# Holding splits and weight work behind evictions, and moving sums and a norm, in a hybrid GLA, mLSTM and ConvFFN layer

## The chip, the cores and the metric

One core of a Trainium2 chip runs the whole layer. The metric is device microseconds of one execution, the median of several runs. Beside the runs there is one profiled execution with a trace of every engine: TensorE (PE, with its weight loads PEld), VectorE (DVE), ScalarE (ACT), GpSimd (POOL) and SyncE (SP), whose queue issues most DMAs.

## The reference

One decoder layer over 1024 tokens and 16 prepended learned tokens, 1024 channels, in float32:

```python
def mixer_block(h, w_in, b_in, ...):
    proj = h @ w_in + b_in
    (g_q, g_k, g_v, g_r, g_lr, m_q, m_k, m_v, m_o, m_i, m_f, gate_a, gate_b) = split(proj)
    o_gla = head_rms(gla_chunked(g_q, g_k, g_v, log_a), gla_norm) * silu(g_r)        # 4 heads
    o_ml = head_rms(mlstm_chunked(mq, mk, m_v, m_i, log_sigmoid(m_f)), ml_norm) * sigmoid(m_o)  # 4 heads
    y = sigmoid(gate_a) * (o_gla @ w_branch_gla) + sigmoid(gate_b) * (o_ml @ w_branch_ml)
    return y @ w_out

def conv_ffn(h, w_up, conv_w, conv_b, w_down):
    gate, up = split(causal_dwconv(h @ w_up, conv_w, conv_b))
    return (silu(gate) * up) @ w_down

h = h + mixer_block(rms_norm(h, norm_mix), ...)
h = h + conv_ffn(rms_norm(h, norm_ffn), ...)
return rms_norm(h, norm_final)[:, N_META:, :]
```

## The kernel before

**Precision and products.** Every float32 operand of a matmul is held as two parts: H, a rounded copy made by ScalarE (`activation(h, raw, AF.Copy)`), and L, the remainder made by VectorE (`tensor_tensor(l, raw, h, subtract)`). This pair of instructions is called a split here. A product takes three matmuls, H·H, H·L and L·H. The gate, up and down stages also save one product in eight with a scheme of sums of blocks: seven products of half size stand for eight, and their operands are sums and differences of blocks of tokens and of weights.

**Stages in order.** (1) Norm and transposes of x. (2) Eight heads s = 0..7 (four GLA, four mLSTM); a head's projections are interleaved on PE with the chunk steps of the head before, its products with v are evicted by VectorE at L205, its output rows go through `post(s, ...)`. (3) The gate stage, 14 weight pairs q = 0..13, two token halves p = 0, 1 each. (4) The merge, with the branch weights (bg, bm). (5) The output projection (po). (6) The up stage, 22 weight pairs. (7) The down stage, two rounds r of two phases. (8) The final norm, per round, and the stores of the output.

**What sets an order.** The program is written as Python that emits instructions. Each engine runs its own list in order; a scheduler makes that list from the order in the program, from when operands are expected, and from priorities (`hp(...)`). `tc.issue_after(ins)` adds an edge: what is emitted inside it comes after `ins` in the list. A tile with a tag takes one of `bufs` places of that tag; a new tile waits until the last reader of the old one in its place is done.

**The gate stage.** `piece(...)` (L987 on) runs one half p of a pair: products V and X into two PSUM banks, evicted by ScalarE L1003 (V into g1) and VectorE L1004 (X + g1); products Y and Z; a second product into the same bank X, evicted by ScalarE L1011 (u2) and added by VectorE L1012 and L1013; then products into Y and Z again, L1018 and L1019. It is a generator: the caller puts the tail of one piece behind the first products of the next. `gate_weights(q)` (L1043 and L1060 to L1067) loads two weight tiles gw and makes sums and splits of them in four steps, called by `weights_step`. `token_blocks` loads the four token blocks TB for both halves p from DRAM (tsc); `token_splits(p)` (L1099, L1100) splits them. In before `token_splits(1)` and the first step of weights q = 1 are emitted between the pieces of q = 0, without an edge.

**The merge.** The eight tiles of o_gla are loaded and split into ogH, ogL by `load_o` (L1192, L1193). The branch weights come through the prefetcher `U`, whose `get` calls `prep` (L102 load, L106 and L107 split), whenever it is that the scheduler finds room.

**The up stage.** `combos(i)` (L1340 to L1357) makes, for the i-th quarter of tokens, combinations t12 and t34 of eight rows each and splits them into BH and BL tiles (Br for blocks, Bt for combinations). The last, i = 3, is emitted while the first pieces already run. `gate_pair(q)` (L1427 to L1439) does the convolution and the product silu(gate)·up, and stores a and its sums s to DRAM (adr).

**The down stage.** `fill(i, ...)` (L1588 transfers in one chain on SP, L1609 and L1610 splits) brings step i's weights (raw, and sums from tdn) and rows (adr) into one of several places; `down` (L1630) runs 24 or 18 matmuls on them. `middle` and `finish` add the banks into accs at L1697; `finish` also squares (L1711), takes roots (VectorE L1715 and L1716, GpSimd L1718), scales with the final norm (L1723) and stores (L1725).

**The token sums.** `token_sums(k)` (L464 to L472) makes, for k = 0..3 during heads s = 3..6, the sums of the token blocks that the gate stage needs: full rows of H + L, their differences, all on GpSimd, then eight DMAs from GpSimd's queue to tsc. It is called at the end of `post(s)`, with rows a and b in tag "r" and t in tag "of". `half_load` and `half_sums` (L485 to L493), which follow, make sums of the down weights. The root of head s, the tile rs{s}r, is a power on GpSimd (L93); ScalarE's scaling of the head's output (L568, L569) waits for it.

Of the kernel before, what the change touches and what calls it, by code (L numbers as in the profile page):

```python
# [45 lines left out]
def hybrid_kernel(ctx, tc, x, meta, norm_mix, w_in, b_in, gla_w_gate, gla_b_gate, gla_norm,  # L46
# [47 lines left out]
        return r  # L94


    behind = []

    def prep(src, shape, name):

        raw = wp.tile(shape, F32, name="wr_" + name, tag="wr", bufs=2)
        nc.sync.dma_start(raw, src)  # L102
        wH = wp.tile(shape, F32R, name="wH_" + name, tag="wH")
        wL = wp.tile(shape, F32R, name="wL_" + name, tag="wL")
        with tc.issue_after(behind[0].ins) if behind else nullcontext():
            nc.scalar.activation(wH, raw, AF.Copy)  # L106
        nc.vector.tensor_tensor(wL, raw, wH.bitcast(F32), OP.subtract)  # L107
        return wH, wL
# [236 lines left out]
    norm_x(0)  # L345
    norm_x(1)
    U.get(0, 0)
    behind.append(norm_x(2)[1])
    U.get(1, 0)
    behind.clear()  # L350
    load_x(3)
    for dst, ap in small[4:9]:
        nc.sync.dma_start(dst, ap)
# [104 lines left out]

    def token_sums(k):

        a, b = (hd.tile([P, T], F32, name=f"x{i}{k}", tag="r", bufs=2) for i in "ab")
        t = hd.tile([P, T], F32, name=f"tx{k}", tag="of", bufs=2)
        for y, i in ((a, k), (b, k + 4)):
            nc.gpsimd.tensor_tensor(y[:, :NP], xH[:, i, T0:].bitcast(F32), xL[:, i, T0:].bitcast(F32), OP.add)  # L464
        first, second = slice(0, 514), slice(512, NP)
        t1, t2 = t[:, 0:514], t[:, 520:1034]
        for dst, x, y in ((t1, a[:, second], a[:, first]), (t2, b[:, second], t1),
                          (a[:, second], b[:, second], a[:, second]), (b[:, first], b[:, first], t2)):
            nc.gpsimd.tensor_tensor(dst, x, y, OP.subtract)
        for i, src in enumerate((t1, t2, a[:, second], b[:, first])):  # L470
            for p in range(2):
                stored = nc.gpsimd.dma_start(tsc[p][i, :, k], src[:, 258 * p:258 * p + 258 - 2 * p])  # L472
        return stored
# [90 lines left out]
    def post(s, o, om, sc, ncols):  # L564

        h = s % 4
        g = "g" if s < 4 else "m"
        for c in range(NC):  # L568
            nc.scalar.activation(o(c), o(c), AF.Copy, scale=sc[:, c + 1:c + 2])  # L569
        nc.scalar.activation(om, om, AF.Copy, scale=sc[:2, 0:1])  # L570
        for _ in range(3 if s != 3 else 6):
            yield
        for j in range(2):
            of = hd.tile([P, T], F32, name=f"of{s}_{j}", tag="r", bufs=2)
            for gi in range(2):
# [12 lines left out]
        if 3 <= s < 7:  # L588
            for _ in range(4 if s == 3 else 0):
                yield  # L590
            stored = token_sums(s - 3)
            if s < 6:
                for _ in range(2):
                    yield
                with tc.issue_after(stored.ins):
                    t = half_load(wp, "gst")
                for _ in range(3):
                    yield
                half_sums(*t)

    def state(name):
# [377 lines left out]
    def product(out, a, b, n, start, stop):  # L981
        for k in range(4):
            for j, (x, y) in enumerate(((a[0], b[0]), (a[0], b[1]), (a[1], b[0]))):
                nc.tensor.matmul(out[:, :n], x[:, k, :], y[:, k, :], start=start and k == 0 and j == 0,  # L984
                                 stop=stop and k == 3 and j == 2, skip_group_check=True)

    def piece(pool, name, p, us_, u2, A, B):  # L987
# [12 lines left out]
        prod(V, "A12", "B21", True, True)  # L1000
        prod(X, "A11", "B11", True, True)
        with hp(PRI_E):
            nc.scalar.activation(g1, V[:, :n], AF.Copy)  # L1003
            nc.vector.tensor_tensor(g1, X[:, :n], g1, OP.add)  # L1004
        yield
        prod(Y, "S1", "T1", True, True)
        prod(Z, "S3", "T3", True, True)
        yield
        prod(X, "S2", "T2", False, True)
        with hp(PRI_E):  # L1010
            nc.scalar.activation(u2, X[:, :n], AF.Copy)  # L1011
            nc.vector.tensor_tensor(e2, Y[:, h2], u2[:, h2], OP.add)  # L1012
            nc.vector.tensor_tensor(e2, Z[:, h2], e2, OP.add)  # L1013
# [81 lines left out]
    def token_splits(p):  # L1095
        c = (slice(0, W0), slice(W0, 514))[p]
        for i in (0, 2, 1, 3):
            h, l = (t[:, :, c] for t in TB[i])
            nc.scalar.activation(h, l.bitcast(F32), AF.Copy)  # L1099
            nc.vector.tensor_tensor(l, l.bitcast(F32), h.bitcast(F32), OP.subtract)  # L1100
# [42 lines left out]
    for q in range(NG):  # L1143
        gu[q] = [row(f"gu0{q}", "u0", 2), row(f"gu1{q}", "o1" if q >= NK and q % 2 else "u1")]
        for p in range(2):
            g = piece(psG, f"g{q}", p, gu[q], u2, WP[q], gate_block)
            next(g)
            if p == 1:
                weights_step(q + 1)
            next(g)  # L1150
            if p == 1:
                weights_step(q + 1)
            if behind_:
                next(behind_)
            if p == 0:
                weights_step(q)
                if q:
                    gate_finish(q - 1)
                else:
                    token_splits(1)  # L1160
                weights_step(q + 1)
# [20 lines left out]
    def load_o(g, pool, tags, queue):  # L1182
# [6 lines left out]
        for k in range(NK):  # L1189
            h, l = (t[p, k // 4][:, k % 4, :NP] for p in "HL")  # L1190
            last = queue.dma_start(l.bitcast(F32), otd[g][k])
            nc.scalar.activation(h, l.bitcast(F32), AF.Copy)  # L1192
            nc.vector.tensor_tensor(l, l.bitcast(F32), h.bitcast(F32), OP.subtract)  # L1193
        return tuple([t[p, k // 4][:, k % 4, :] for k in range(NK)] for p in "HL"), last

    ubg = [u_cm(w_bg, P * j, f"bg{j}") for j in range(NK)]
    ubm = [u_cm(w_bm, P * j, f"bm{j}") for j in range(NK)]
# [25 lines left out]
        nc.gpsimd.dma_start(yg[j], gsc["a"][j])  # L1223

    merge_tile(0)
    og, loaded = load_o("g", r2, "O", nc.gpsimd)
    for j in range(NK):
        y = yg[j]
        if j < NK - 1:
# [4 lines left out]
            nc.vector.tensor_tensor(th(y), pt, th(y), OP.mult)  # L1234
        if j == 1:
            with tc.issue_after(opened.ins), tc.issue_after(loaded.ins):
                om_, loaded = load_o("m", r1b, "R", nc.gpsimd)
        for i in ((), (), (5, 6, 7), (6, 7), (6, 7), (), (), ())[j]:
            half_sums(*half_load(r2, f"Y{i}"))

# [103 lines left out]
    def combos(i):  # L1344
# [6 lines left out]
        nc.vector.tensor_tensor(t12[:, 4:8], B[:, 4:8], t12[:, 0:4], OP.subtract)  # L1351
        nc.vector.tensor_tensor(t34[:, 0:4], B[:, 4:8], B[:, 0:4], OP.subtract)
        nc.vector.tensor_tensor(t34[:, 4:8], A[:, 4:8], t12[:, 4:8], OP.subtract)
        for dst, r0, n, src in ((Br, 0, 8, A), (Br, 8, 4, B[:, 4:8]), (Bt, 0, 8, t12), (Bt, 8, 8, t34)):
            h = dst["H", p][:, r0:r0 + n, c0:c0 + w]
            nc.scalar.activation(h, src, AF.Copy)
            x = nc.vector.tensor_tensor(dst["L", p][:, r0:r0 + n, c0:c0 + w], src, h.bitcast(F32), OP.subtract)  # L1357
# [347 lines left out]
    def finish(r, j):  # L1705
# [21 lines left out]
        with hp(400 if j == 0 else 200):  # L1727
# [8 lines left out]
            if not end:  # L1736
# [37 lines left out]
            if (r, ph, m) == (1, 0, 1):  # L1774
                ring.extend(back)

    back = []
    i = FIRST
    while i < len(seq):
        r, ph, m = seq[i]  # L1780
# [53 lines left out]
```

## Time and profile before

| | us |
|---|---|
| runs | 1926.53, 1923.99, 1923.37 |
| median | 1923.99 |
| profiled execution, its own time | 1925.63 |
| its span from first to last instruction | 1923.6 |
| mean granted clock of TensorE | 0.995 |

How to read what follows. A row of the timeline is: start in us, duration in us, engine, line, operation, output<-input, partitions x elements, xcount, and in brackets how long the engine sat idle before it and who released it. A row of the waits is: who waited, for whom, us in total, times, longest. A row of windows is: start:end, length, PE's busy time with its matmuls, the granted clock of TensorE (1.00 is full), the DMA engines' share, GB/s. An engine with a q behind its name (SPq, ACTq) is issuing a DMA.

### The profile page before, as it was taken

What the parts mean: (1) busy time and instruction counts of PE and PEld (TensorE: products, weight loads), DVE (VectorE), ACT (ScalarE), POOL (GpSimd) and SP (SyncE); (2) the same over time, 40 slices, a digit from 0 to 9 for tenths busy, and PEclk for the clock granted to TensorE, in tenths of its full rate; (3) what the DMA queues carried; (4) which work ended last, traced back from release to release, by engine and by line L of the source; (5) the groups of instructions that cost most, each with busy time, mean ns of one, the idle gap of its engine ahead of it and who ended that gap; (6) DMA issues with size and microseconds to landing.
All of it is one profiled execution on the core that took longest, in us unless ns stands there. A gap on an engine that the chain in (4) does not pass through costs nothing. (4 is left out here: it accounts for less than half of the span.)

```text
span 1923.6 us, 32692 instructions
## 1 busy us (share of the span) xinstructions
PE 1867.8 (97%) x13377; PEld 1785.1 (93%) x13377; DVE 1199.3 (62%) x1775; ACT 853.9 (44%) x1369; POOL 413.5 (21%) x463
## 2 busy tenths in 40 slices
PE   8999999999999899999899999999999999999998
PEld 8989989999889899999899999999999999987776
DVE  6456556455552356565442555688888788886776
ACT  5345555545453433332331234544343443455564
POOL 3101111140553001124272610012222222200000
PEclk9999999999999999999999999999999999999999
DMA  5111021042332936666873653323433334288794
GB/s 166 34 36 58 12 69 50 20 136 91 99 100 89 212 84 165 165 167 174 286 260 112 219 177 121 123 79 108 129 119 100 106 109 127 82 305 332 265 369 161
DMA packets 221824, 270.02 MB, mean 140 GB/s; under 512 B 13742, under 2 KB 177088, under 8 KB 221675
## 3 DMA queue, kind: packets, MB, share of 16 engines
q1 hardware_dynamic: 200603, 199.93, 33.5%
q0 software_dynamic: 16928, 57.76, 9.2%
q10 hardware_dynamic: 4144, 10.26, 1.5%
q8 instruction: 105, 1.72, 0.4%
q14 instruction: 44, 0.36, 0.1%
HBM read 198.33 MB, written 69.57 MB: 139 GB/s over the span
## 5 line engine op out<-in xcount | busy, mean ns | idle before, releaser
L491 POOL TENSOR_TENSOR ts<-ts 128x256 f32<-128x256 f32 x88 | 75.6, 866 | 43.0 <-DMA ts<-in_ffn_w_down_dram 41.0
L1394 POOL TENSOR_TENSOR SB<-SA,rg 128x512 f32<-128x512 f32 x20 | 31.8, 1591 | 236.6 <-issue 123.7
L201 PE MATMUL pv<-wH_gv,xH 128*128 128x256 f32 x256 | 75.3, 294 | 0.0
L201 PE MATMUL pv<-wH_mv,xH 128*128 128x256 f32 x256 | 75.1, 293 | 0.0
L1481 PE MATMUL po<-wH_wo,yH 128*128 128x256 f32 x256 | 72.8, 284 | 0.1
L201 PE MATMUL pv<-wH_gv,xL 128*128 128x256 f32 x256 | 72.5, 283 | 0.0
L201 PE MATMUL pv<-wL_gv,xH 128*128 128x256 f32 x256 | 72.1, 282 | 0.0
L1481 PE MATMUL po<-wL_wo,yH 128*128 128x256 f32 x256 | 71.7, 281 | 0.3 <-DVE wL_wo L107 0.3
L1481 PE MATMUL po<-wH_wo,yL 128*128 128x256 f32 x256 | 72.0, 282 | 0.0
L201 PE MATMUL pv<-wL_mv,xH 128*128 128x256 f32 x256 | 72.0, 281 | 0.0
L201 PE MATMUL pv<-wH_mv,xL 128*128 128x256 f32 x256 | 71.9, 281 | 0.0
L704 POOL TENSOR_TENSOR pk<-pk,kT 128x256 f32<-128x256 f32 (+1 forms) x24 | 30.6, 1277 | 175.0 <-ACT pk L702 164.4
L1209 PE MATMUL bg<-ogH,wH_bg 128*128 128x342 f32 x192 | 61.8, 323 | 3.9 <-ACT ogH L1192 3.9
L1429 DVE SCALAR_TENSOR_TENSOR cv<-u,fc,cv 128x1024 f32<-128x1024 f32 x44 | 65.3, 1483 | 0.4
L1376 POOL TENSOR_TENSOR A<-u2raw,A 128x512 fp32r<-128x512 f32 x20 | 43.9, 2195 | 92.5 <-ACT A L1375 92.5
L1209 PE MATMUL bg<-ogL,wH_bg 128*128 128x342 f32 x192 | 61.9, 324 | 0.7 <-DVE ogL L1193 0.7
L1209 PE MATMUL bg<-ogH,wL_bg 128*128 128x342 f32 x192 | 61.8, 323 | 0.0
L1209 PE MATMUL bm<-omH,wH_bm 128*128 128x342 f32 x192 | 61.4, 320 | 0.0
L1209 PE MATMUL bm<-omH,wL_bm 128*128 128x342 f32 x192 | 61.3, 319 | 0.0
L1209 PE MATMUL bm<-omL,wH_bm 128*128 128x342 f32 x192 | 61.2, 319 | 0.0
L205 DVE TENSOR_TENSOR v<-pv,bB 128x256 f32<-128x256 f32 x64 | 26.8, 419 | 54.4 <-PE pv L201 54.3
L1718 POOL TENSOR_TENSOR fr<-fv,mhalf 128x1 f32<-128x1 f32 x8 | 6.4, 806 | 231.9 <-DVE fv L1716 231.9
(754 smaller groups left out, 7508.9 us busy)
## 6 DMA issues: line engine op xcount, KB each, us to landing
gw<-in_w_in_dram SPq DMA_DIRECT2D x26, 512.0 KB
ts<-in_ffn_w_down_dram POOLq DMA_DIRECT2D x44, 256.0 KB, 3.6
tdn<-ts POOLq DMA_DIRECT2D x44, 256.0 KB, 2.8
rg<-in_ffn_w_up_dram SPq DMA_DIRECT2D x22, 512.0 KB
ru<-in_ffn_w_up_dram SPq DMA_DIRECT2D x22, 512.0 KB
adr<-s SPq DMA_DIRECT2D x40, 256.0 KB
rd<-in_ffn_w_down_dram SPq DMA_DIRECT2D x20, 512.0 KB
do<-tdn SPq DMA_DIRECT2D x18, 512.0 KB
```

The lines of the kernel that those rows point to most:

```text
L201: nc.tensor.matmul(pt[:, :DV], a[:, k, t0:t0 + P], b[:, k % 4, :], start=(i == 0), stop=(i == 3 * NK - 1))
L205: nc.vector.tensor_tensor(vt[:n, c, :DV], pt[:n, :DV], bB[:n, :], OP.add)
L491: nc.gpsimd.tensor_tensor(t[:, o], t[:, a], t[:, b], OP.subtract)
L704: eng.tensor_tensor(e, e, k, OP.mult)
L1209: nc.tensor.matmul(pt[:, i, :n], a[:, k, :], b[k][:, t0:t0 + n], start=(k == 0 and j == 0), stop=(k == NK - 1 and j == 2))
L1376: eng.tensor_tensor(l, src, h.bitcast(F32), OP.subtract)
L1394: late.tensor_tensor(sb[:, 0:4], sa[:, 0:4], rg[:, 0:4], OP.subtract)
L1429: nc.vector.scalar_tensor_tensor(y, u[:, j:SEQ + j], fc[:, j, jj:jj + 1], y, OP.mult, OP.add)
L1481: nc.tensor.matmul(pt[:, :DV], a, b[:, k % 4, :], start=(k == 0 and i == 0), stop=(k == NK - 1 and i == len(terms) - 1))
L1718: nc.gpsimd.tensor_tensor(rs, v, mhalf, OP.pow)
```

## The change

It moves work in time; the arithmetic is the same.

- The list `behind` becomes `held`, set by `hold(...)`; `prep` puts the first half of a split after the held instruction.
- `piece` remembers its evictions in `evicted` (V: L1003, X: L1004, U: L1011, Z: L1013 by the lines of before).
- Gate stage: `token_splits(1)` is cut in two. Blocks 0 and 2 come after the evictions of V and X of the first piece, blocks 1 and 3 and the first step of weights q = 1 after U and Z; the next steps of q = 1 also after Z.
- Merge: the second use of the branch-weight prefetcher comes after the last U, the third after the last split of o_gla.
- Up stage: `combos(3)` makes six splits in place of four, in another order.
- From up to down: `fill(0)` comes after the last U.
- Token sums: two rows in tag "of" in place of two in "r" and one in "of"; eight operations of 514 columns in place of two of 1026 and four of 514; called at the start of `post(s)`. The half loads and half sums go into the loop over j.
- Final norm: roots, scaling and stores of round 0 are put off to step k = 2 of the next phase.

```diff
+    held = []
+    def hold(*ins):
+        held[:] = ins
     def prep(src, shape, name):
...
-        with tc.issue_after(behind[0].ins) if behind else nullcontext():
+        with tc.issue_after(held[0]) if held else nullcontext():
             nc.scalar.activation(wH, raw, AF.Copy)
...
     def token_sums(k):
-        a, b = (hd.tile([P, T], F32, name=f"x{i}{k}", tag="r", bufs=2) for i in "ab")
-        t = hd.tile([P, T], F32, name=f"tx{k}", tag="of", bufs=2)
-        for y, i in ((a, k), (b, k + 4)):
-            nc.gpsimd.tensor_tensor(y[:, :NP], xH[:, i, T0:].bitcast(F32), xL[:, i, T0:].bitcast(F32), OP.add)
...
+        a, b = ([t[:, :514], t[:, 520:1034]] for t in (
+            hd.tile([P, T], F32, name=f"x{i}{k}", tag="of", bufs=2) for i in "ab"))
+        def whole(dst, i, c0):
+            nc.gpsimd.tensor_tensor(dst, xH[:, i, c0:c0 + 514].bitcast(F32), xL[:, i, c0:c0 + 514].bitcast(F32), OP.add)
+        def less(dst, x, y):
             nc.gpsimd.tensor_tensor(dst, x, y, OP.subtract)
+        whole(a[1], k, second)
+        whole(a[0], k, first)
+        less(b[0], a[1], a[0])
+        whole(b[1], k + 4, second)
+        less(a[1], b[1], a[1])
+        less(b[1], b[1], b[0])
+        whole(a[0], k + 4, first)
+        less(a[0], a[0], b[1])
...
     def post(s, o, om, sc, ncols):
+        if 3 <= s < 7:
+            stored = token_sums(s - 3)
         for c in range(NC):
...
                 if gi == 0:
                     yield
+                    if 3 <= s < 6:
+                        if j == 0:
+                            with tc.issue_after(stored.ins):
+                                t = half_load(wp, "gst")
+                        else:
+                            half_sums(*t)
...
-        if 3 <= s < 7:
-            for _ in range(4 if s == 3 else 0):
-                yield
-            stored = token_sums(s - 3)
...
             if p == 0:
                 weights_step(q)
                 if q:
                     gate_finish(q - 1)
+                    weights_step(q + 1)
                 else:
-                    token_splits(1)
-                weights_step(q + 1)
+                    with tc.issue_after(evicted["V"]), tc.issue_after(evicted["X"]):
+                        token_splits(1, (0, 2))
             next(g)
+            if p == 0 and q == 0:
+                opening = dict(evicted)
+                with tc.issue_after(evicted["U"]), tc.issue_after(evicted["Z"]):
+                    token_splits(1, (1, 3))
+                    weights_step(1)
...
     merge_tile(0)
-    og, loaded = load_o("g", r2, "O", nc.gpsimd)
+    og, loaded, split = load_o("g", r2, "O", nc.gpsimd)
+    hold(evicted["U"])
+    U.get(ubg[0], 1)
+    hold(split.ins)
+    U.get(ubg[0], 2)
+    hold()
...
+        if i == 3:
+            jobs = ((Br, 0, 8, A), (Bt, 0, 4, t12[:, 0:4]), (Bt, 8, 4, t34[:, 0:4]), (Bt, 4, 4, t12[:, 4:8]),
+                    (Br, 8, 4, B[:, 4:8]), (Bt, 12, 4, t34[:, 4:8]))
...
             used[i] = ring[i](i)
-            fill(i, used[i])
+            with tc.issue_after(evicted["U"]) if i == 0 else nullcontext():
+                fill(i, used[i])
...
             if not end:
-                whole(1)
+                if r:
+                    whole(1)
+                else:
+                    later.append(whole)
                 return
...
+        if later and k == 2:
+            for whole in later:
+                for x in range(2):
+                    whole(x)
+            later.clear()
```

More of the change, by code (lines that the diff above doesn't have):

```diff
@@ L94, in rstd_of @@
         return r
-    behind = []
+    held = []
+    def hold(*ins):
+        held[:] = ins
     def prep(src, shape, name):
@@ L347, in hybrid_kernel @@
     U.get(0, 0)
-    behind.append(norm_x(2)[1])
+    hold(norm_x(2)[1].ins)
     U.get(1, 0)
-    behind.clear()
+    hold()
     load_x(3)
@@ L459, in token_sums @@
     def token_sums(k):
-        a, b = (hd.tile([P, T], F32, name=f"x{i}{k}", tag="r", bufs=2) for i in "ab")
-        t = hd.tile([P, T], F32, name=f"tx{k}", tag="of", bufs=2)
-        for y, i in ((a, k), (b, k + 4)):
-            nc.gpsimd.tensor_tensor(y[:, :NP], xH[:, i, T0:].bitcast(F32), xL[:, i, T0:].bitcast(F32), OP.add)
[L465 to L470, printed above, removed]
+        a, b = ([t[:, :514], t[:, 520:1034]] for t in (
[3 more added lines that the diff above has]
+        def less(dst, x, y):
+            nc.gpsimd.tensor_tensor(dst, x, y, OP.subtract)
+        first, second = T0, T0 + 512
+        whole(a[1], k, second)
[6 more added lines that the diff above has]
+        less(a[0], a[0], b[1])
+        for i, src in enumerate((b[0], b[1], a[1], a[0])):
             for p in range(2):
@@ L587, in post @@
             yield
-        if 3 <= s < 7:
-            for _ in range(4 if s == 3 else 0):
-                yield
-            stored = token_sums(s - 3)
[L592 to L599, printed above, removed]
     def state(name):
@@ L985, in product @@
                                  stop=stop and k == 3 and j == 2, skip_group_check=True)
+    evicted = {}
     def piece(pool, name, p, us_, u2, A, B):
@@ L1002, in piece @@
         with hp(PRI_E):
-            nc.scalar.activation(g1, V[:, :n], AF.Copy)
-            nc.vector.tensor_tensor(g1, X[:, :n], g1, OP.add)
+            evicted["V"] = nc.scalar.activation(g1, V[:, :n], AF.Copy).ins
+            evicted["X"] = nc.vector.tensor_tensor(g1, X[:, :n], g1, OP.add).ins
         yield
@@ L1010, in piece @@
         with hp(PRI_E):
-            nc.scalar.activation(u2, X[:, :n], AF.Copy)
+            evicted["U"] = nc.scalar.activation(u2, X[:, :n], AF.Copy).ins
             nc.vector.tensor_tensor(e2, Y[:, h2], u2[:, h2], OP.add)
-            nc.vector.tensor_tensor(e2, Z[:, h2], e2, OP.add)
+            evicted["Z"] = nc.vector.tensor_tensor(e2, Z[:, h2], e2, OP.add).ins
         yield
@@ L1093, in token_blocks, with token_splits @@
                 nc.sync.dma_start(TB[i][1][:, :, c].bitcast(F32), tsc[p][i])
-    def token_splits(p):
+    def token_splits(p, blocks=(0, 2, 1, 3)):
         c = (slice(0, W0), slice(W0, 514))[p]
-        for i in (0, 2, 1, 3):
+        for i in blocks:
             h, l = (t[:, :, c] for t in TB[i])
@@ L1147, in hybrid_kernel @@
             next(g)
-            if p == 1:
-                weights_step(q + 1)
-            next(g)
-            if p == 1:
-                weights_step(q + 1)
+            for again in (True, False):
+                if p == 1:
+                    with nullcontext() if q else tc.issue_after(opening["Z"]):
+                        weights_step(q + 1)
+                if again:
+                    next(g)
             if behind_:
@@ L1191, in load_o @@
             last = queue.dma_start(l.bitcast(F32), otd[g][k])
-            nc.scalar.activation(h, l.bitcast(F32), AF.Copy)
+            split = nc.scalar.activation(h, l.bitcast(F32), AF.Copy)
             nc.vector.tensor_tensor(l, l.bitcast(F32), h.bitcast(F32), OP.subtract)
-        return tuple([t[p, k // 4][:, k % 4, :] for k in range(NK)] for p in "HL"), last
+        return tuple([t[p, k // 4][:, k % 4, :] for k in range(NK)] for p in "HL"), last, split
     ubg = [u_cm(w_bg, P * j, f"bg{j}") for j in range(NK)]
@@ L1225, in hybrid_kernel @@
     merge_tile(0)
-    og, loaded = load_o("g", r2, "O", nc.gpsimd)
+    og, loaded, split = load_o("g", r2, "O", nc.gpsimd)
[3 more added lines that the diff above has]
+    U.get(ubg[0], 2)
+    hold()
     for j in range(NK):
@@ L1236, in hybrid_kernel @@
             with tc.issue_after(opened.ins), tc.issue_after(loaded.ins):
[L1237 removed]
+                om_, loaded, _ = load_o("m", r1b, "R", nc.gpsimd)
         for i in ((), (), (5, 6, 7), (6, 7), (6, 7), (), (), ())[j]:
@@ L1353, in combos @@
         nc.vector.tensor_tensor(t34[:, 4:8], A[:, 4:8], t12[:, 4:8], OP.subtract)
-        for dst, r0, n, src in ((Br, 0, 8, A), (Br, 8, 4, B[:, 4:8]), (Bt, 0, 8, t12), (Bt, 8, 8, t34)):
+        jobs = ((Br, 0, 8, A), (Br, 8, 4, B[:, 4:8]), (Bt, 0, 8, t12), (Bt, 8, 8, t34))
+        if i == 3:
+            jobs = ((Br, 0, 8, A), (Bt, 0, 4, t12[:, 0:4]), (Bt, 8, 4, t34[:, 0:4]), (Bt, 4, 4, t12[:, 4:8]),
+                    (Br, 8, 4, B[:, 4:8]), (Bt, 12, 4, t34[:, 4:8]))
+        for dst, r0, n, src in jobs:
             h = dst["H", p][:, r0:r0 + n, c0:c0 + w]
@@ L1735, in finish @@
             square(0, 1)
-            if not end:
+            if not end and r:
                 whole(0)
@@ L1775, in ahead @@
                 ring.extend(back)
-    back = []
+    back, later = [], []
     i = FIRST
```

2 lines of the change are left out of this document (1 added, 1 removed).

## The prediction

> **What bounds the kernel now.** I read the page first, then TensorE's waits, then the granted clock behind the longest of them, and last the timelines of the stages that the change touches.
>
> ```profile
> span 1923.6 us, 32692 instructions
> PE 1867.8 (97%) x13377; PEld 1785.1 (93%) x13377; DVE 1199.3 (62%) x1775; ACT 853.9 (44%) x1369; POOL 413.5 (21%) x463
> ```
>
> TensorE (PE) is busy 97% of the span and the change neither adds nor removes a matmul. All that a new order can win is its 1923.6 - 1867.8 = 55.8 us of idle time and whatever matmuls ran at a lowered clock. The waits of PE (us in total, times, longest):
>
> ```profile
> PE Xg L984 <- DVE gu L1004: 9.2, 2, 8.1
> PE bg L1209 <- ACT ogH L1192: 3.9, 1, 3.9
> PE op L917 <- DVE om L902: 3.8, 2, 2.8
> PE pdV L1630 <- DVE db L1610: 3.4, 2, 2.9
> PE Yu L984 <- DVE u L1012: 2.2, 1, 2.2
> PE Yu L984 <- ACT BH1t L1356: 2.2, 1, 2.2
> PE Yg L984 <- DVE gu L1012: 1.1, 1, 1.1
> PE pe L158 <- ACT gu L1011: 1.0, 1, 1.0
> PE op L917 <- DVE dn L920: 0.8, 2, 0.6
> ```
>
> Every one of these lies at a place where the change moves something. Some of the waits leave a second cost behind; PEclk is the column after PE's busy time:
>
> ```profile
> 676.70:679.30 2.60, 2.60 (x12) 0.50 0.00 0
> 1259.80:1263.00 3.20, 3.20 (x17) 0.50 0.03 5
> 1690.80:1693.70 2.90, 2.90 (x24) 1.00 1.02 405
> ```
>
> After the 8.1 us wait and after one of the two 2.2 us waits TensorE ran about 3 us at half clock, so about 1.3 us and 1.6 us are lost beyond the waits; after the other 2.2 us wait it did not.
>
> **The opening of the gate stage.** The second product into bank X needs X evicted (VectorE L1004), and L1004 needs V evicted (ScalarE L1003).
>
> ```profile
> 667.48 2.20 ACT L1099 ACTIVATE TH<-TL 128x1024 fp32r<-128x1024 f32 x2 [4.25 <-DMA TL<-tsc]
> 672.29 0.39 ACT L1003 ACTIVATE gu<-Vg 128x258 f32<-128x258 f32 x1 [0.40 <-ACT gb L453]
> 676.15 0.42 DVE L1004 TENSOR_TENSOR gu<-Xg,gu 128x258 f32<-128x258 f32 x1
> 717.47 0.69 DVE L1060 TENSOR_TENSOR gS<-gw,gw 128x512 f32<-128x512 f32 x1 [6.42 <-DMA gw<-in_w_in_dram]
> ```
>
> ScalarE stood 4.25 us before token splits whose data had not landed, with V's eviction queued behind them; VectorE then did the next weights' combinations before L1004. In the changed order both evictions come first, so the second X product follows without a wait: -8.1 for the wait, -1.3 for the clock, together **-9.4**. What is late next is the split of the second token half and the weights of q=1. The first two blocks land at 667.48 as before and are needed only when four more products have run; the held weights are ready some 2 us ahead of their product when I step through the new order with these durations. The loads of later weights start behind splits of these buffers, so the wait at 717.47 (9.2 - 8.1 = 1.1 us of PE) stays and might grow: end of the range -7.
>
> **The opening of the merge.** In before the second branch weight is split ahead of the last evictions, the third ahead of the last gate bank:
>
> ```profile
> 930.83 1.06 ACT L106 ACTIVATE wH_bg<-wr_bg 128x1024 fp32r<-128x1024 f32 x1 [3.23 <-DMA wr_bg<-in_w_branch_gla_dram]
> 931.79 0.36 ACT L1011 ACTIVATE gu<-Xg 128x256 f32<-128x256 f32 x1
> 931.91 1.23 DVE L107 TENSOR_TENSOR wL_bg<-wr_bg,wH_bg 128x1024 fp32r<-128x1024 f32 x1 [3.06 <-ACT wH_bg L106]
> 933.72 0.41 DVE L1012 TENSOR_TENSOR gu<-Yg,gu 128x256 f32<-128x256 f32 x1
> 947.91 1.06 ACT L106 ACTIVATE wH_bg<-wr_bg 128x1024 fp32r<-128x1024 f32 x1 [3.23 <-PE pe L158]
> ```
>
> With the splits behind them, L1011 starts about 0.6 us earlier and L1012 stands behind neither 1.23 us nor the three evictions that queued up behind it, which clears the 1.1 us wait of Yg. The third split (947.91) stood ahead of an eviction, the sigmoid and the first ogH split that bg waits for; without it that chain starts about 0.8 us sooner, and 3.1 of the 3.9 us stay. -0.6 - 1.1 - 0.8 = **-2.5** (-1.5 to -3.5). The third weight, now split behind eight og splits, is first needed tens of us later.
>
> **The opening of the up stage.** Eight-row splits become four-row ones in another order.
>
> ```profile
> 1257.69 1.22 DVE L1357 TENSOR_TENSOR BL1r<-hT,BH1r 128x1024 fp32r<-128x1024 f32 x1
> 1257.81 1.06 ACT L1356 ACTIVATE BH1t<-T 128x1024 fp32r<-128x1024 f32 x1 [3.71 <-DVE T L1351]
> ```
>
> The first matmuls of Yu and Zu may now run inside the old wait, but the third of the order, Vu, needs BL1r, and that VectorE still ends at 1257.69 + 1.22 = 1258.91, where the old wait ended. So the wait shrinks by only 0.3 us. The gain is the clock: idle time falls into pieces of about 1.7 us in all, less than the 2.2 us that kept full clock elsewhere. -0.3 - 1.6 = **-1.9**; with the half clock still there -0.3.
>
> [...]
>
> **From up to down.** fill(0) goes behind the eviction of the last piece.
>
> ```profile
> 1688.08 1.06 ACT L1609 ACTIVATE dy<-dy 128x1024 fp32r<-128x1024 f32 x1 [5.92 <-DMA dy<-tdn]
> 1689.17 1.23 DVE L1610 TENSOR_TENSOR dy<-dy,dy 128x1024 fp32r<-128x1024 f32 x1 [1.55 <-ACT dy L1609]
> 1691.78 1.06 ACT L1609 ACTIVATE dw<-dy 128x1024 fp32r<-128x1024 f32 x1 [2.37 <-DMA dy<-adr]
> 1693.74 0.39 PE L1630 MATMUL pdV<-dy,dw 128*128 128x512 f32 x1
> ```
>
> ScalarE's eviction loses its 0.5 us behind dy, VectorE's L1012 its 0.9 us behind the 1.23 us subtraction: 1.4 of the 2.2 us. But the first pdV needs the split that ends at 1691.78 + 1.06 = 1692.84 and is bound to a landing. PE, which came to it at 1693.74, now comes at 1692.3, so 0.5 us comes back as a wait: **-0.9**. The rest of that fill and the last activations come later on both engines; their loads were far ahead. Ends: +1 (a fill late once by about one 1.06 us split) and -2.2 (the whole wait).
>
> **The closing norm of the first half.**
>
> ```profile
> 1806.66 1.06 ACT L1609 ACTIVATE db<-db 128x1024 fp32r<-128x1024 f32 x1 [0.89 <-DMA db<-adr]
> 1813.98 1.29 DVE L1723 SCALAR_TENSOR_TENSOR accs<-accs,fr,gfin 128x1024 f32<-128x1024 f32 x1 [0.44 <-POOL fr L1718]
> 1816.44 1.22 DVE L1610 TENSOR_TENSOR db<-db 128x1024 fp32r<-128x1024 f32 x1
> ```
>
> PE waits 2.9 us for the db of 1816.44, whose ScalarE half was done at 1807.72; in between VectorE waited for roots and scaled rows. In the new order the db splits precede all roots and can end near 1809, before PE wants them: **-2.9**. The four L1723 and the four stores still run; the stores move behind loads in SP's queue, two of them between the accs loads that wait for them. Those accs are added only at the end of the phase. Ends -2 to -2.9, and see the last rival.
>
> **The token sums.** The same elements and 32 DMAs, but each head's chain now stands in GpSimd's queue ahead of the head's root (L93) and runs beside other VectorE work.
>
> ```profile
> 371.95 0.59 PE L805 MATMUL op<-v,An 128*128 128x256 f32 x2
> 380.43 3.79 POOL L93 TENSOR_TENSOR rs3r<-rs3v,mhalf 128x9 f32<-128x9 f32 x1 [7.23 <-DVE rs3v L91]
> 383.88 0.42 DVE L205 TENSOR_TENSOR v<-pv,bB 128x256 f32<-128x256 f32 x1
> 484.50 1.27 POOL L469 TENSOR_TENSOR tx<-xa 128x514 f32<-128x514 f32 x1
> 494.84 2.28 POOL L469 TENSOR_TENSOR xa<-xb,xa 128x514 f32<-128x514 f32 x1
> 497.06 0.56 POOL L472 DMA_DIRECT2D tsc<-tx  x1
> 506.12 0.59 PE L917 MATMUL op<-v,wt 128*128 128x257 f32 x2
> 514.38 1.83 POOL L93 TENSOR_TENSOR rs5r<-rs5v,mhalf 128x9 f32<-128x9 f32 x1 [2.90 <-DVE rs5v L91]
> ```
>
> A 514-column operation takes 1.27 us alone and 2.28 us beside VectorE. In the first head the second row is free after the matmul of 371.95, at 372.5; six operations and four DMA issues of 0.56 us end at 372.5 + 7.6 + 2.2 = 382.3, or 388.4 contended, so the root starts 2 to 8 us late. [...] I take +3.5 (0 to +6). Third head: from 506.7 the six operations and all eight issues take 7.6 + 4.4 us and some contention, root near 521 instead of 514.38, an eviction queued behind the work on that root: +2.6 (0 to +4). Second and fourth head: mostly covered, +0.3. Against that the waits of the old places go: -3.8 and -0.8. Together **+1.8** (-4.6 to +7).
>
> **Sum.** -9.4 - 2.5 - 1.9 - 0.9 - 2.9 + 1.8 = -15.8. The profiled execution took 1925.63 us (span plus 2.0), so 1909.8; it was 1.6 above the median, and I say **1910**.
>
> **Rivals.** (a) The sums cost their upper end, +7 instead of +1.8: every head's root late with ScalarE's scaling and the transposes behind it. For it: evictions without slack in the first head. Against: three heads have other work for PE. 1915. (b) The gate stage gives only half back: PE, 9.4 us earlier, meets the weight load of 717.47 sooner and pays there. For: VectorE already waits 6.42 us for it. Against: that load starts behind splits that move with PE. 1910 + 4.7 = 1915. (c) Slower: the roots behind the sums in all four heads. If a head's output chain holds the next head by the root's whole lateness, about 8 us, four heads cost 32 instead of the 6.4 in the sum: 1935. It turns the sign from (15.8 + 6.4) / 4 = 5.6 us a head on. Against: most of the next head's work does not wait for this head's root. (d) The holds change nothing, since every held thing was waiting for a landing anyway: 1924. Against: the instruction orders do differ at every one of the named waits.
>
> **How the numbers follow.** Forecast 0.53, (a) 0.17, (b) 0.12, (c) 0.12, (d) 0.06. What can be told from no change is 0.2%, 3.8 us. The first three are faster, 0.82; (d) makes 0.06 the same and (c) 0.12 slower. Low end: the ends of the gate, merge, up-to-down and sums terms together are some 9 us below 1910, 1901. High end: (a) and (b) at 1915 plus half of what would add if both came, 1920; beyond it lie (c), (d) and little else.
>
> **What would show it.** Right: no wait of Xg longer than 1.1 us, full clock at 676 and 1260, bg's wait near 3 us, no wait before the last Yu over 1 us, none of pdV over 1 us at the middle of down; the waits of op for om gone and new, shorter ones of PE for v or dn near heads three and five, with L93 2 to 8 us later in its head. Wrong: a wait of several us for gw at 680 to 720, or ot and op waiting for the roots in more than two heads.

## The result and the profile after

The changed kernel takes 1909.37 us (median of four runs, 1907.36 to 1911.00) against 1925.26 us (four runs, 1923.37 to 1927.13). The ratio is 0.9917, 95% interval 0.9900 to 0.9934: 15.9 us less where 15.8 were forecast, 1909.4 us where 1910 was. The page of the profiled execution (its own time 1907.36 us) opens so:

```profile
span 1905.4 us, 32685 instructions
PE 1863.9 (98%) x13377; PEld 1783.5 (94%) x13377; DVE 1208.6 (63%) x1777; ACT 853.3 (45%) x1371; POOL 418.0 (22%) x471
```

The span is 18.2 us shorter: PE is idle 14.3 us less (55.8 to 41.5) and busy 3.9 us less with the same 13377 matmuls. Of the 3.9 us, 1.4 lie at the start of the kernel, which the change does not touch; the half clock of the gate and the up stage is gone (1.6 and 1.1 us less), and one in the heads is new (1.8 us more). The main waits of PE in the changed kernel at the places that the change moves, with its own line numbers (L990 was L984, L208 was L205, L1020 was L1012, L1224 was L1209):

```profile
PE pj L161 <- DVE v L208: 4.8, 2, 2.4
PE bg L1224 <- ACT ogH L1207: 3.0, 1, 3.0
PE Yg L990 <- DVE gu L1020: 1.7, 1, 1.7
PE pv L204 <- DVE v L208: 1.5, 1, 1.5
PE Vu L990 <- DVE BL1r L1381: 1.1, 1, 1.1
PE Yu L990 <- DVE u L1020: 1.0, 1, 1.0
PE pe L161 <- ACT gu L1019: 0.5, 1, 0.5
PE Zu L990 <- ACT BH1t L1380: 0.2, 1, 0.2
```

The 8.1 us of Xg and the 2.9 us of pdV are gone; so are both waits of op, but three new ones for v (L208), 6.3 us in all, stand in the heads. The wait of Xg at the later weight load (1.1 us) has given way to one of Yg one pair earlier (1.7 us).

To see where the time went, the span is cut at the ends of seven waits that every kernel below has: ot in the last head, pe, bg (its first matmul), htp, the last Yu of the up stage, and the first pdZ wait of each round. Lengths in us, from one profile each:

| kernel | start to ot | to pe | to bg | to htp | to last Yu | to pdZ, round 0 | to pdZ, round 1 | to end |
|---|---|---|---|---|---|---|---|---|
| before | 637.9 | 294.3 | 19.7 | 285.9 | 453.0 | 67.5 | 110.8 | 54.5 |
| changed | 639.5 | 284.6 | 17.5 | 286.2 | 450.0 | 65.6 | 107.5 | 54.5 |
| changed, again | 642.4 | 284.0 | 17.5 | 286.0 | 450.0 | 66.2 | 107.6 | 54.5 |
| gate opening undone | 638.7 | 293.7 | 17.5 | 286.6 | 451.5 | 65.6 | 107.6 | 54.4 |
| merge holds undone | 639.6 | 284.9 | 19.6 | 286.7 | 450.1 | 65.6 | 109.1 | 54.4 |
| up splits undone | 641.0 | 283.0 | 17.5 | 286.1 | 450.2 | 66.3 | 107.5 | 54.5 |
| first fill undone | 640.9 | 285.6 | 17.5 | 287.2 | 452.1 | 67.9 | 107.6 | 54.5 |
| final norm undone | 641.1 | 284.7 | 17.5 | 286.2 | 450.0 | 67.3 | 109.2 | 54.5 |
| final norm undone, again | 640.9 | 283.5 | 17.5 | 286.4 | 450.0 | 65.6 | 109.5 | 54.5 |
| sums undone | 637.5 | 285.4 | 17.5 | 286.1 | 450.0 | 66.5 | 107.5 | 54.5 |
| sums held | 638.4 | 284.2 | 17.5 | 286.0 | 451.5 | 65.8 | 107.5 | 54.5 |
| first head late, others held | 632.6 | 285.5 | 17.5 | 286.9 | 450.0 | 66.2 | 107.8 | 54.5 |

The gate column (to pe) gives 9.7 us, the merge 2.2, up 3.0 (1.2 of it at the last Yu, where the fill stood), the first round 1.9, the final norm 3.3. The heads cost 1.6 on paper, but the start of the kernel happened to be 1.4 us quicker in this profile: from the same matmul near 371 us to ot they cost 3.0.

### The profile page after: what moved, and what is told of

Read it like the earlier page. It is cut to its first block, busy times and chain, and to the rows that moved or that the text cites. A ratio compares the mean times of both kernels' runs of the same rounds, so it can differ in the third digit from the quotient of the medians.

```text
span 1905.4 us, 32685 instructions
## 1 busy us (share of the span) xinstructions
PE 1863.9 (98%) x13377; PEld 1783.5 (94%) x13377; DVE 1208.6 (63%) x1777; ACT 853.3 (45%) x1371; POOL 418.0 (22%) x471
## 5 line engine op out<-in xcount | busy, mean ns | idle before, releaser
L502 POOL TENSOR_TENSOR ts<-ts 128x256 f32<-128x256 f32 x88 | 82.4, 941 | 50.2 <-DMA ts<-in_ffn_w_down_dram 47.9
L1224 PE MATMUL bg<-ogH,wH_bg 128*128 128x342 f32 x192 | 61.9, 324 | 3.0 <-ACT ogH L1207 3.0
L1224 PE MATMUL bg<-ogL,wH_bg 128*128 128x342 f32 x192 | 61.9, 324 | 0.7 <-DVE ogL L1208 0.7
L1224 PE MATMUL bg<-ogH,wL_bg 128*128 128x342 f32 x192 | 61.9, 323 | 0.0
L1224 PE MATMUL bm<-omH,wH_bm 128*128 128x342 f32 x192 | 61.4, 320 | 0.0
L1224 PE MATMUL bm<-omH,wL_bm 128*128 128x342 f32 x192 | 61.3, 319 | 0.0
L1224 PE MATMUL bm<-omL,wH_bm 128*128 128x342 f32 x192 | 61.2, 319 | 0.0
L208 DVE TENSOR_TENSOR v<-pv,bB 128x256 f32<-128x256 f32 x64 | 26.6, 419 | 51.5 <-PE pv L204 51.5
```

The costliest lines, as they stand in the source:

```text
L208: nc.vector.tensor_tensor(vt[:n, c, :DV], pt[:n, :DV], bB[:n, :], OP.add)
L502: nc.gpsimd.tensor_tensor(t[:, o], t[:, a], t[:, b], OP.subtract)
L1224: nc.tensor.matmul(pt[:, i, :n], a[:, k, :], b[k][:, t0:t0 + n], start=(k == 0 and j == 0), stop=(k == NK - 1 and j == 2))
```

## The experiments

Unless said otherwise, each is the changed kernel with one edit; the diffs show the lines that matter. A ratio is to runs of the kernel before that stand beside the runs in question; their median lay between 1921.74 and 1925.26 us, so a difference of 2 or 3 us between the times of two variants is not shown by the times alone.

**The changed kernel again** (no edit).

> The changed kernel once more, unaltered, for its clock. [...] Rival (half clock belongs to a place of the program, such as the instructions around it): half clock again at 386 to 391 us and at 943 to 947 us and nowhere else in the middle.

1910.18 us (four runs, 1906.96 to 1912.49; ratio 0.9930, 0.9908 to 0.9951). Windows of PE in the first profile and then in the second; the number after the matmuls is the granted clock:

```profile
387.00:390.00 3.00, 3.00 (x12) 0.50 0.46 155
524.00:527.00 3.00, 3.00 (x19) 1.00 0.08 27
526.00:529.00 3.00, 3.00 (x21) 1.00 0.43 121
```

```profile
387.00:390.00 3.00, 2.27 (x14) 1.00 0.28 93
526.00:529.00 3.00, 3.00 (x12) 0.50 0.09 11
```

The waits listed above are the same to 0.1 us (a new one of 0.6 us, pj for kT, and two smaller ones come or go), but half clock now follows the second 2.4 us wait and not the first. It does not belong to a place of the program. Other profiles below have it after both (up splits undone) or for about 6.8 us after bg (first fill undone, 944.6 to 951.4 us).

**Gate opening undone.**

```diff
-                    with tc.issue_after(evicted["V"]), tc.issue_after(evicted["X"]):
-                        token_splits(1, (0, 2))
+                    token_splits(1)
...
```

The steps of the weights q = 1 go back to their old places and lose their edges too.

> The opening of the gate stage as before, all else as changed. Theory: the 8.1 us wait of Xg for VectorE's L1004 comes back with about 1.3 us of half clock behind it, so about 9.4 us slower than the changed kernel, 1918 to 1920 us; from the start of the gate stage to its last product the distance is that of before. Rival (PE meets the later weight loads in any case and the opening wins only half): slower by 4 to 6 us, with waits of PE for weight loads of q = 2 and 3 gone.

1917.67 us (ten runs; ratio to before 0.9967, 0.9956 to 0.9977), 8.3 us above the first four runs of the changed kernel and 7.5 above the second four. Two of PE's waits, and a window behind each:

```profile
PE Xg L990 <- DVE gu L1012: 8.4, 1, 8.4
PE Vu L990 <- DVE BL1r L1374: 1.1, 1, 1.1
```

```profile
675.50:681.00 5.50, 2.63 (x12) 0.50 0.04 17
1259.00:1262.00 3.00, 3.00 (x16) 0.50 0.00 0
```

The wait is back with its half clock, 9.1 us in its column, of which 0.8 is a wait of pc ahead of the gate stage (1.1 us here, 0.3 in the changed kernel). The half-win rival falls in size, since the loss is not 4 to 6 us. Its sign came all the same: neither the old wait of Xg for weights (1.1 us) nor the one of Yg (1.7 us) is in this profile. In the ten other profiles of this table with the new opening Yg waits 0.4 to 1.8 us there, so about that much of the gain is paid back where PE comes sooner to the weights (in the changed kernel VectorE stands 3.33 us for their landing at 690.63 us). The second window holds a surprise: here the up stage ran at half clock after the 1.1 us wait of Vu, which the changed kernel's profile passed at full clock.

**Merge holds undone.**

```diff
-    hold(evicted["U"])
-    U.get(ubg[0], 1)
-    hold(split.ins)
-    U.get(ubg[0], 2)
-    hold()
```

> The branch weights' splits not held, all else as changed. Theory: pe waits 1.0 us for L1011, Yg 1.1 us for L1012 and bg 3.9 us for ogH again, 2.2 us more from the wait of pe to the first bg matmul than in the changed kernel (19.7 us in place of 17.5 us). Rival (the wait of bg is set by the landing of o_gla or the gate rows, not by the splits): bg waits 3.0 us as now and the stretch is under 1.2 us longer.

One run, 1911.72 us.

```profile
PE bg L1224 <- ACT ogH L1207: 3.9, 1, 3.9
PE Yg L990 <- DVE gu L1020: 2.5, 2, 1.5
PE pe L161 <- ACT gu L1019: 0.5, 1, 0.5
```

bg waits 3.9 us again and one of the two Yg waits (1.0 us) is the old one: 2.1 us in the column. The wait of pe was expected back at 1.0 us and stays at 0.5, so that part of the gain (0.5 us) is not the merge's.

**Up splits undone.**

```diff
-        if i == 3:
+        if False:
             jobs = ((Br, 0, 8, A), (Bt, 0, 4, t12[:, 0:4]), ...
```

> The last combinations of the up stage split as before (four splits), all else as changed. [...] Rival (the six splits themselves save 2 us or more): the stage from the first Yu of the second half to the products of the next pair is over 1.5 us longer at full clock.

One run, 1908.29 us.

```profile
PE Yu L990 <- ACT BH1t L1380: 2.2, 1, 2.2
```

The old 2.2 us wait is back, this time at full clock, and the stage is 0.2 us longer. The six splits themselves win 0.2 us.

**First fill undone.**

```diff
-            with tc.issue_after(evicted["U"]) if i == 0 else nullcontext():
-                fill(i, used[i])
+            fill(i, used[i])
```

> The first fill of the down stage not held, all else as changed. Theory: the last Yu waits 2.2 us for L1012 (VectorE) again in place of 1.0 us, and the small waits of pdV for db and dy near steps 8 and 10 of the down stage (0.5 and 0.7 us) come back, because the stores of the last activations and the loads behind them return to their old place: 1.2 to 2.5 us slower from the last up product to the end of the first round. Rival (the hold only moves the wait): the sum of waits between the last up product and the first round's end is unchanged within 0.5 us.

One run, 1915.14 us.

```profile
PE Yu L990 <- DVE u L1020: 3.1, 1, 3.1
PE pdV L1654 <- ACT dy L1633: 0.6, 1, 0.6
PE pdV L1654 <- DVE db L1634: 0.5, 1, 0.5
PE pdV L1654 <- ACT db L1633: 0.3, 1, 0.3
```

The last Yu waits 3.1 us in place of 1.0, and the small waits of pdV are back: 2.1 + 2.3 us in the two columns, more than the 1.2 to 2.5 expected. The rest of this run's distance lies outside them, in clock and landings. The rival falls: the hold removes waits and moves none. But of the small ones only those for db are the hold's. They are in no profile that has it, while pdV waits 0.3 to 1.4 us for dy in five profiles that have it.

**Final norm undone**, profiled twice.

```diff
-                    later.append(whole)
+                whole(1)
```

(and `whole(0)` at its old place without the condition on r)

> Roots, scaling and stores of the first round right behind its sums as before, all else as changed. Theory: pdV waits 2.9 us for VectorE's db in the middle of the down stage, and nothing else changes: the distance from the first round's last matmul to the end of the kernel grows by 2.9 to 3.3 us. Rival (moving the stores later costs the second round as much in DMA as it wins): the distance changes by less than 1 us.

> The first round's roots, scaling and stores right behind its sums once more, because the first look showed 1.3 us of wait in the middle where the kernel before had 2.9. Theory (what VectorE waits for there is a square on ScalarE, queued behind a split of a load; when the load lands decides between 1.3 and 2.9 us): the wait differs again between the looks, anywhere from 1 to 3 us, by as much as the landing of that load moves. Rival (the changed order around it fixes 1.3 us): 1.2 to 1.4 us again, with the load landing before ScalarE comes to it.

1912.13 and 1909.94 us, one run each. The waits of pdV in the first, then in the second profile:

```profile
PE pdV L1654 <- ACT dy L1633: 1.4, 1, 1.4
PE pdV L1654 <- DVE db L1634: 1.3, 1, 1.3
```

```profile
PE pdV L1654 <- DVE db L1634: 1.7, 1, 1.7
```

The wait is back, but as 1.3 and 1.7 us, and the second round is 1.7 and 2.0 us longer, not 2.9 or more: not the number of either theory. ScalarE in the kernel before, then in the first and in the second profile, around the load that the squares queue behind:

```profile
1810.54 1.06 ACT L1609 ACTIVATE do<-rd 128x1024 fp32r<-128x1024 f32 x1 [2.81 <-DMA rd<-in_ffn_w_down_dram]
1811.50 0.61 ACT L1711 ACTIVATE sqj<-accs 128x512 f32<-128x512 f32 x1
```

```profile
1797.40 1.06 ACT L1633 ACTIVATE do<-rd 128x1024 fp32r<-128x1024 f32 x1 [2.21 <-DMA rd<-in_ffn_w_down_dram]
1798.36 0.62 ACT L1736 ACTIVATE sqj<-accs 128x512 f32<-128x512 f32 x1
```

```profile
1794.92 1.06 ACT L1633 ACTIVATE do<-rd 128x1024 fp32r<-128x1024 f32 x1 [2.53 <-DMA rd<-in_ffn_w_down_dram]
1795.89 0.61 ACT L1736 ACTIVATE sqj<-accs 128x512 f32<-128x512 f32 x1
```

In all three the root's squares stand behind the split of a load that ScalarE waits for (2.81, 2.21 and 2.53 us). The db that PE needs comes 6.2 us after these squares start in each: PE asks for it 3.3, 4.9 and 4.6 us after them and waits 2.9, 1.3 and 1.7 us. So the chain is equally long in all three, and when the load lets it start decides how much of it PE sees. In the changed kernel VectorE does not stand behind those squares:

```profile
1791.03 2.35 DVE L1634 TENSOR_TENSOR db<-db 128x1024 fp32r<-128x1024 f32 x2
1798.77 1.28 DVE L1748 SCALAR_TENSOR_TENSOR accs<-accs,fr,gfin 128x1024 f32<-128x1024 f32 x1 [0.59 <-POOL fr L1743]
```

The 1.4 us of dy in the first profile is in the first round, before the edited place, and is absent in the second: a landing too.

**Sums undone** (`token_sums` and `post` as before the change).

> Token sums, half loads and half sums as before, all else as changed. Theory (the new place of the sums costs more than the old one): the three waits of pj and pv for v's evictions, 6.3 us in all, and the half clock behind the first go, the old waits of op for om and dn, 4.5 us, come back; 2 to 4 us faster than the changed kernel, 1906 to 1907 us. Rival (the sums are neutral or better in their new place): within 1 us of the changed kernel or slower.

1906.88 us (four runs; ratio 0.9914, 0.9892 to 0.9937). The waits of op:

```profile
PE op L920 <- DVE om L905: 3.7, 2, 2.8
PE op L920 <- DVE dn L923: 0.8, 2, 0.6
```

So the new place of the sums costs about 2.5 us net by the medians. The profiles say it more surely: counted from the same matmul near 371 us to ot, the eight profiles with the new place take 2.8 to 4.3 us more than the kernel before, this one 0.1 less. In the changed kernel these are 6.3 us of new waits and one stretch of half clock for 4.5 us of old waits. In the changed kernel the first head shows this on VectorE and GpSimd (the same scan, `sr<-sr,raw_s`, took 2.31 us before):

```profile
376.21 3.31 DVE L526 TENSOR_TENSOR_SCAN sr<-sr,raw_s 4x1040 f32<-4x1040 f32 x1
383.03 2.13 DVE L838 SCALAR_TENSOR_TENSOR kc<-kT,col,kc 128x1040 f32<-128x1040 f32 x1
385.08 0.41 DVE L208 TENSOR_TENSOR v<-pv,bB 128x256 f32<-128x256 f32 x1
```

```profile
381.15 2.92 POOL L471 TENSOR_TENSOR xa<-xa,xb 128x514 f32<-128x514 f32 x1
385.13 1.83 POOL L93 TENSOR_TENSOR rs3r<-rs3v,mhalf 128x9 f32<-128x9 f32 x1
```

The row work before the eviction of 385.08 is stretched, and the root starts at 385.13 in place of 380.43. In the third head PE's wait hangs on the root:

```profile
521.46 1.84 POOL L93 TENSOR_TENSOR rs5r<-rs5v,mhalf 128x9 f32<-128x9 f32 x1
```

```profile
523.33 0.17 DVE L937 TENSOR_TENSOR rs5r<-rs5r,rc 128x9 f32<-128x9 f32 x1 [4.45 <-POOL rs5r L93]
523.41 0.75 DVE L208 TENSOR_TENSOR v<-pv,bB 128x256 f32<-128x256 f32 x2
```

VectorE stands 4.45 us at a 9-column product that needs the root, and the eviction that PE waits for is next in its queue. The root is late for two reasons. Its input is late, because four small operations of VectorE ahead of it are stretched by the sums; before, then in the changed kernel:

```profile
511.40 1.14 DVE L845 SCALAR_TENSOR_TENSOR wt<-MB,tcol,big 128x128 f32<-128x128 f32 x4
```

```profile
511.63 5.35 DVE L851 SCALAR_TENSOR_TENSOR wt<-MB,tcol,big 128x128 f32<-128x128 f32 x4
```

The input is done at 518.74 us in place of 514.29, 4.4 us late. Then the root waits another 2.7 us for GpSimd, behind the last issues of the sums and two of the half load. The fourth head shows the same: 4.92 us in place of 1.14 for these operations, an input 3.9 us late and 1.0 us more in GpSimd's queue.

**Sums held behind the root.**

```diff
-            stored = token_sums(s - 3)
+            with tc.issue_after(roots[f"rs{s}"]):
+                stored = token_sums(s - 3)
```

(`rstd_of` keeps its GpSimd instruction in `roots`)

> The changed kernel with each head's token sums also put behind that head's root in GpSimd's queue, by an edge. Theory (the loss in the heads is the sums standing ahead of the root and beside VectorE's row work): the root of the third GLA-to-mLSTM head is on time again (ScalarE's wait for it back from 5.0 to about 2.1 us), the 2.4 us wait near 385 us goes or shrinks below 1 us, and the kernel is 2 to 6 us faster than the changed one. Rival (only the contention of GpSimd and VectorE matters, wherever the sums stand): waits of the same 6 us in all appear some 10 us later in each head, the time stays within 2 us.

1907.28 us (five runs, 1906.44 to 1916.87; ratio 0.9930, 0.9906 to 0.9953). By the median 2 to 3 us under the changed kernel, but the ratio is that of its second four runs, so a gain in time is not shown. Two of the waits from 375 to 400 us, the first head:

```profile
PE pj L163 <- DVE v L210: 3.0, 2, 2.6
ACT or L585 <- POOL rs3r L95: 2.1, 1, 2.1
```

In the first head the root is on time again (ScalarE waits 2.1 us, as before, and not 5.0), yet PE waits 2.6 + 0.4 us for v, some 5 us later than in the changed kernel. The expectation was under 1 us. There the sums beside VectorE's row work cost, not a late root: from 383.7 us on three row operations take 1.70, 2.23 and 2.20 us in place of 0.69, 1.30 and 1.23. In the third and fourth head the waits of 2.4 and 1.5 us are gone. This doesn't tell GpSimd's queue from the stretched operations: behind the root the sums also miss those, and they take 1.14 us again in the third head.

**First head late, others held.** The first head's sums, half load and half sums as before the change, the sums of the next three heads held behind their roots:

```diff
+        if 4 <= s < 7:
+            with tc.issue_after(roots[f"rs{s}"]):
+                stored = token_sums(s - 3)
...
+        if s == 3:
+            for _ in range(4):
+                yield
+            stored = token_sums_late(0)    # three rows, tags "r", "r", "of"
```

> The changed kernel with the first head's sums made as before the change (three rows, behind the head's output) and those of the next three heads put behind their roots by an edge. Theory (each head's sums are free of cost where they run beside no eviction that PE is waiting for: for the first head that is its old place, for the other three the place right behind the root): no wait over 0.5 us in heads 3 to 7, 1903 to 1905 us, faster than the changed kernel by 4 to 6 us and than the two single variants by 2 to 3. Rival (the sums' work costs about the same wherever it stands): waits of 3 us or more in the heads, 1906 us or more.

1901.10 us (five runs, 1900.03 to 1902.96; ratio 0.9883, 0.9865 to 0.9902), the fastest of all. All waits of PE from 370 to 660 us:

```profile
PE pc L163 <- ACT gb L458: 1.4, 1, 1.4
PE ot L610 <- ACT of L612: 0.9, 1, 0.9
PE otm L622 <- DVE KT L902: 0.3, 1, 0.3
```

The first stands behind the heads and the second in the last one, as in the other kernels; the sums' own waits are down to 0.3 us. It is 8.3 us under the changed kernel by the medians, 6.5 by the ratios (9 against the second four runs), more than the 4 to 6 expected: 6.3 us of waits and the half clock that followed them.

## Why the prediction was right

The time and the main mechanism held: the largest term of the sum was the opening of the gate stage, and undoing that alone gives about half of the gain back. That forecast and result agree to 0.1 us is luck. Of the up term 1.6 us are not shown to be the order's, the terms from up to down and of the sums were off by 2.2 and 1.2 us in opposite directions, the forecast starts from one profile of 1925.63 us, and the runs of the changed kernel spread over 3.6 us. By its steps:

- **Gate, -9.4.** Held in its mechanism, and a little less in size: 9.7 us in its column, with 0.5 us of pe's wait that the sum had in the merge; 9.1 us in it when undone, 0.8 of that from pc; 8.3 us by the medians. The 1.1 us wait for weights that the prediction kept came as 1.7 us one pair earlier. V's eviction runs at 665.61, X's at 667.11, no wait follows:

```profile
665.61 0.39 ACT L1011 ACTIVATE gu<-Vg 128x258 f32<-128x258 f32 x1 [0.97 <-PE Vg L990]
667.11 0.43 DVE L1012 TENSOR_TENSOR gu<-Xg,gu 128x258 f32<-128x258 f32 x1 [4.85 <-PE Xg L990]
```

- **Merge, -2.5.** Held: 2.2 us in its column and 0.5 at pe, which undoing it does not bring back; 3.0 us of the bg wait stayed, 3.1 by the forecast.
- **Up, -1.9.** The order part was right (0.3 forecast, 0.2 measured, and the wait did move to BL1r). The clock part, 1.6 us, is not shown to be the order's: the stage ran at half clock in two of the ten profiles that have the new splits (gate opening undone, sums held) and in one of the two that have the old ones. The row "full clock after 2.2 us elsewhere" did not bear the weight I put on it: the last section has pairs of waits of one length with half clock behind one of them alone.
- **From up to down, -0.9.** Too small: 1.2 us at the last Yu and 1.9 us in the first round, 3.1 together; undone, 4.4. The 0.5 us that I gave back to the landing did not come, and I had not priced the second effect, the waits of pdV for db (0.5 us before) that went. That the fills' loads no longer stand behind the last activations' stores may be the reason; it is not shown. The 0.7 us for dy is a landing's, since profiles with the hold have such a wait too.
- **Final norm, -2.9.** The wait vanished and the column shows 3.3 us, but in the undone kernel it is 1.7 and 2.0 us: the mechanism is right, and the size depends on a landing, which in the profile of before left PE the shortest lead. The same column shows 109.1 us once with the norm put off (merge holds undone), where pdV waits 1.2 us for another db.
- **Token sums, +1.8.** Right in sign and too small: 3.0 us in this profile, 2.8 to 4.3 in all eight. In the first head the root was 4.7 us late, within the 2 to 8 written. No run shows the 3.5 us in the form in which it was put there; what the runs showed in its place is 2.4 us of wait and 1.8 us of half clock in that head, with the scan at 3.31 us in place of 2.31 and the product after it (kc, L838) at 2.13 in place of 1.30. In the third the root came at 521.46 us, near 521 as forecast, but GpSimd's queue made only 2.7 us of its lateness; the 4.4 us of VectorE's stretched operations were not in the sum of that head. The fourth head was mis-sized: its 1.5 us wait had been put at 0.3 together with the second. The costs of both kinds were larger than written, 6.3 us and a half clock against 6.4 without one. (The upper end of +7 is more than its own pieces give: 6 + 4 + 0.3 - 4.6 = 5.7.)

Rival (a), the sums at +7, and (b), half a gate gain, did not come, though the evictions that (a) named were short of slack (TensorE's weight load waits 0.2 us for one of them in the kernel before); (c) needed a head's lateness to pass on in full, while in the first head the root starts 4.7 us late and PE has no wait behind it until the third head. (d) fell with the wait of Xg.

In the first head the lengths show the two engines side by side. From 371.28 us, with VectorE idle up to 374.76, three 514-column operations of GpSimd took 1.30 to 1.31 us each; beside VectorE's row work the next three took 2.33, 2.52 and 2.92. On VectorE the scan took 3.31 us in place of 2.31, while the eviction between the scans (379.55 us) took 0.43 us, as in the kernel before.

## What to carry to other kernels

When a bank's eviction stands behind work on its engine that still waits for data, look at the engine's order before its load: moving two evictions ahead was worth more here than any other part. A chain moved to an otherwise idle engine cost here where it stretched its neighbour's operations (1.14 to 5.35 us for four small ones in the third head) and where something urgent stood behind it in the same queue (2.7 us for that head's root). Putting it behind the urgent instruction can cure both at once, as in two heads here, and then does not tell them apart: read from the trace when the urgent instruction's input was ready and when it started. Price idle time on TensorE with a possible half-clock stretch behind it (1.1 to 1.8 us here), but do not credit an order with a clock that another profile of the same kernel may not show.

## What the runs showed of the hardware that was not expected

Half clock moved between two profiles of one kernel with the same waits (386 us in one, 526 us in the other), and a stretch of it cost 1.1 to 1.8 us (1.6 in the gate stage, 1.1 in the up stage and 1.8 in the heads by PE's busy time, 1.5 in the up column with the gate opening undone); the runs of the changed kernel spread over 3.6 us.

The length of a wait alone did not tell whether half clock follows. In the changed kernel PE waited 2.42 us up to 385.55 us and 2.43 us up to 523.88; half clock followed the first, from 386.67 to 390.08 us, and not the second. In the kernel before it waited 2.21 us for the up stage's Yu, up to 1258.92 us, and 2.23 us for the last Yu, up to 1690.79; half clock followed the first, from 1259.83 to 1263.24 us, and not the second.

Each of these two stretches lasted 3.41 us. In the kernel before half clock lasted 6.82 us around the end of the 8.1 us wait (672.74 to 679.56 us, with 2.93 us of matmuls in it), and after bg it lasted about 6.8 us in two profiles (first fill undone; first head late, others held); the windows of the kernel with the first fill undone:

```profile
945.00:948.40 3.40, 3.05 (x11) 0.50 1.11 369
948.40:951.80 3.40, 3.40 (x15) 0.56 0.95 319
```
